# One fixed TensorE order for the RWKV stage of a hybrid recurrent layer on Trainium2, and weight splits of 1024 columns

## The chip, the cores and the metric

The kernel runs on one core of a Trainium2 chip. The metric is the device time of one launch in microseconds (us): the median of 3 runs was 2476.36 us (2475.43 to 2477.71).

Engine names follow the profile: PE is TensorE (matmuls), PEld its weight loads, DVE is VectorE, ACT ScalarE, POOL GpSimd, SP the queue that issues the DMAs. Each engine takes its instructions in the order in which they were laid down when the kernel was built, and an instruction that waits holds back those behind it.

## What is computed

One step of a decoder layer for 320 token rows: 256 rows of a prompt and 8 samples of 8 rows. Cut to what matters:

```
h    = rmsnorm(x)                     # 320 x 2048
proj = h @ w_in                       # 2048 -> 4096 (HGRN) + 3328 (RWKV) + 3072 (conv) + 6144 (gates)
y_a  = hgrn2(proj[:, HGRN]) @ w_pa
y_b  = rwkv7(proj[:, RWKV]) @ w_pb    # 16 heads of 64
y_c  = (sb * conv3(sc * sh)) @ w_pc   # short gated convolution
m    = sum of sigmoid(gates) * (y_a, y_b, y_c)
x1   = x + rmsnorm(m @ w_o)
y    = x1 + rmsnorm(relu(rmsnorm(x1) @ w_ff1)^2 @ w_ff2)     # 2048 -> 8192 -> 2048
```

The RWKV-7 part is a recurrence over the tokens of each head, S_t = S_{t-1} (diag(w_t) - kk_t (a_t kk_t)^T) + v_t k_t^T with o_t = S_t r_t, followed by a group norm, a bonus term and a gate. Besides y the step returns the new states.

## The kernel before

**Dense work.** All of it is held with features on the partitions and the 320 rows on the free axis. fp32 products are made from rounded halves: `split` (L103 to L105) writes the high part of a tile on ScalarE and the remainder on VectorE. `granule` (L107) loads 512 KB of weights (128 x 1024) on the SP queue and splits them in two halves of 512 columns; raw weights, high parts and low parts have three buffers each. `dense` (L118) accumulates one tile of 128 x 320 outputs in PSUM: for each block of 128 input features three matmuls (L128 to L130: high x high, high x low, low x high). A projection, `proj`, is 16 such blocks from two granules, 48 matmuls.

**Order of the work.** A scheduler orders each engine's instructions when the kernel is built: it takes, of those that are ready by its own account of time, the one that was written first. So program order is a priority, and the order on the chip comes from the scheduler's account. In the stage described next this decides between dense blocks, which are nearly always ready, and short matmuls of dependent chains.

**The RWKV stage** (`rwkv`, L277) follows the first norm. It works on eight pairs of heads ("heads" below), j = 0 to 7, and for each there are:

- *shift_mix* (L253): three projections (k, r, v) with a mix of each row and the row before it; two more projections serve all heads.
- *front* (L333): a low-rank product for the decay and the gate a (L346), the running product of decays in each chunk of 64 rows, a sum of squares by a matmul (L368) with `rsqrt` (L161 to L166), the operands LYR and BK, then transposes of v into X (L397, L398), the bonus (L408) and the transposes BT (L417).
- *solve* (L423): the products within the chunks (L443), masked by VectorE into Nb, GB and LYR (L452 to L457); a DRAM round trip that gathers the 16 x 16 diagonal blocks on 40 partitions, 15 dependent steps of two VectorE instructions (L474, L476), the way back into Pm (L479), and two levels of transposes and products (L499, L503, L509).
- *chunks* (L513): for each of four chunks of the prompt, one after the other, Y (L543, copied by ScalarE, L546), the solved rows (L551, copied by VectorE, L553) and the next state (L555, scaled by VectorE, L561 and L563); then the same once for the sample rows (L576 to L596).
- *tail*: group norm, transposes of Od (L635), bonus, gate product (L640) and B (L641).

`rwkv` writes them down as front 0, solve 0, front 1, and then for each j: solve j+1, chunks j, `short_conv` tiles by the list `SC_ORDER`, front j+2. `short_conv` (L672) needs three projections per tile. The branch outputs B and Cb (128 x 8 x 320 each) stay in SBUF.

**After the stage** come the HGRN stage with the merges of Cb as filler, the merges of B and A, `out_mix` and the MLP. A merge needs its branch as halves bh and bl, made by `merge_split` (L918); its projection of the gate (16 blocks) comes first.

Of the kernel before, what the change touches and what calls it, by code (L numbers as in the profile page):

```python
# [9 lines left out]
F32 = mybir.dt.float32  # L10
# [73 lines left out]
SC_ORDER = ((), (0,), (1,), (2,), (3,), (4,), (5,), (6, 7))  # L84


class K:
# [19 lines left out]
    def granule(self, src, pool=None):  # L107
# [10 lines left out]
    def dense(self, granules, ah, al):  # L118
# [4 lines left out]
        for g in granules:  # L123
            hi, lo = self.granule(g)
            for k in range(8):
# [5 lines left out]
                i += 1  # L131
        return ps[:, :NT]

# [17 lines left out]
    def proj(self, n):  # L151
        w = self.io["w_in"]
        return self.dense([w[n, 0], w[n, 1]], self.xh, self.xl)

# [15 lines left out]
    def build(self):  # L170
# [46 lines left out]
        bp = self.pool("bo", ctx=xgs)  # L217
        self.B = bp.tile([128, 8, NT], F32, name="B")
        self.Cb = bp.tile([128, 8, NT], F32, name="Cb")
# [11 lines left out]
        self.merge_split(self.Cb)  # L231
# [5 lines left out]
        for src, i, w in ((self.B, 1, io["w_pb"]), (self.A, 0, io["w_pa"])):  # L237
            self.merge_split(src)
# [14 lines left out]
    def shift_mix(self, wp, n, name, packed):  # L253

        nc = self.nc
        ps = self.proj(n)
# [12 lines left out]
        xs = wp.tile([128, NT], F32, name="xs" + name, bufs=2 if name == "v" else 1)  # L269
# [7 lines left out]
    def rwkv(self, cx):  # L277
# [21 lines left out]
        for nm, cols in (("Nb", 640), ("GB0", 640), ("GB1", 640), ("LX", 256), ("Ms", 256), ("Od", 640)):  # L299
# [9 lines left out]
        for d in self.dP:  # L309
            nc.sync.dma_start(d[0:128 * 640].rearrange("(p x) -> p x", x=640), Z["Nb"])  # L310
        self.Z = Z
        xwa = self.shift_mix(w2, RWA, "k", True)
        self.L = kp.tile([128, NT], F32, name="L")
        nc.scalar.activation(self.L[0:64, :], xwa[0:64, :], AF.Tanh)
        nc.scalar.copy(self.L[64:128, :], xwa[64:128, :])
        xg = self.shift_mix(w2, RG, "v", True)
        self.Lg = kp.tile([128, NT], F32, name="Lg")
        nc.scalar.activation(self.Lg, xg, AF.Sigmoid)
# [12 lines left out]
        nc.sync.dma_start(io["o_shift"], self.shl)  # L331

    def rwkv_front(self, j, wp, w2):  # L333
# [5 lines left out]
        kx = self.shift_mix(w2, RK + j, "k", False)  # L339
        r = self.shift_mix(w2, RR + j, "r", False)  # L340
        vx = self.shift_mix(w2, RV + j, "v", True)
# [17 lines left out]
        W = w2.tile([128, NT], F32, name="W")  # L359
        V.tensor_mul(W, Wp, wt[:, 1:])  # L360
        Wi = wp.tile([128, NT], F32, name="Wi")
        V.reciprocal(Wi, W)


        sq = wp.tile([128, NT], F32, name="sq")
# [8 lines left out]
        LYR = w2.tile([128, 5, 4, 64], F32, name="LYR")  # L374
        BK = w2.tile([128, 5, 3, 64], F32, name="BK")
# [12 lines left out]
        S.copy(BK[:, :, 2, :], BK[:, :, 0, :])  # L388
        rk = wp.tile([128, NT], F32, name="rkk")
        V.scalar_tensor_tensor(rk, r, self.par("rk", j), t, ALU.mult, ALU.mult)  # L390


        X = w2.tile([128, 5, 2, 64], F32, name="X")
# [12 lines left out]

        bs = self.pa.tile([128, 512], F32, name="pa_t")
# [3 lines left out]


        BT = w2.tile([128, 5, 2, 64], F32, name="BT")
# [6 lines left out]

        return W, LYR, BK, X, BT, vx

    def rwkv_solve(self, j, front, wp):  # L423
        nc, io = self.nc, self.io
        V, G, S, T = nc.vector, nc.gpsimd, nc.scalar, nc.tensor
        W, LYR, BK, X, BT, vx = front
# [726 lines left out]
```

## Time and profile before

| | |
|---|---|
| median of 3 runs | 2476.36 us |
| profiled execution | 2475.11 us, its span 2473.3 us |
| instructions | 41923 |
| DMA | 354.94 MB, mean 144 GB/s; weights come in 512 KB transfers |
| groups of instructions | L104 on ScalarE 685.8 us of 1192 (mean 618 ns); L105 on VectorE 828.2 us of 1192 (mean 724 ns) |

How to read it: the page gives one profiled execution. A row of the view by lines names line, engine, operation, output and inputs, the shape and the count; then busy time and the mean of one; then the idle time of that engine just before them, and what ended it. A row of the waits says which engine waited at which line for which producer: total us, times, longest. "issue" is time for which the profile shows nothing waited for. Matmuls are pipelined, so one that is listed with 309 ns can be followed by the next after half of that, and the time of a PE row is no measure of what it costs. The page's RWKV stage reaches from about 30 us to 574 us.

### The profile page before, as it was taken

How to read it: one execution, taken by the hardware profiler on the slowest of the kernel's cores; microseconds unless marked ns; L12 is line 12 of the kernel's file. 1: busy time of each engine (PE TensorE's matmuls, PEld its weight loads, DVE VectorE, ACT ScalarE, POOL GpSimd, SP SyncE). 2: the span in 40 equal slices, each digit the busy share in tenths (PEclk: the TensorE clock that was granted, in tenths of full speed). 3: DMA queues.
4: the chain of work that ended last, by engine and by line, in shares of the span. 5: the costliest groups of instructions: out<-in, count | busy, mean ns of one | idle time of the engine just before them, and what ended most of it. 6: DMA issues, size and time to landing. Idle time of an engine off the chain costs nothing.

```text
span 2473.3 us, 41923 instructions
## 1 busy us (share of the span) xinstructions
PE 2425.8 (98%) x16244; PEld 2326.5 (94%) x16244; DVE 1513.2 (61%) x3102; ACT 989.9 (40%) x1919; POOL 384.4 (16%) x536
## 2 busy tenths in 40 slices
PE   8999999999999999999999999999999999999998
PEld 7888888889999999999999897999999999999997
DVE  6878888876565656655555536754555555555555
ACT  5444444434444434433444335344333333333333
POOL 5422332220000011011111334300000000000003
PEclk9999999999999999999999999999999999999999
DMA  6323333334433333344444654444444444444443
GB/s 216 118 89 107 110 116 113 119 120 147 135 136 131 138 131 130 123 155 152 151 148 149 237 180 164 143 152 151 148 152 147 153 148 151 151 148 154 146 153 128
DMA packets 131703, 354.94 MB, mean 144 GB/s; under 512 B 34864, under 2 KB 43440, under 8 KB 131504
## 3 DMA queue, kind: packets, MB, share of 16 engines
q1 hardware_dynamic: 131504, 352.25, 41.3%
q8 instruction: 129, 2.11, 0.3%
q14 instruction: 70, 0.57, 0.1%
HBM read 337.06 MB, written 15.14 MB: 142 GB/s over the span
## 4 chain that ended last, share of the span: by engine, by line
PE 89%; DVE 8%; POOL 1%; issue 1%; ACT 1%; DMA 0%; SPq 0%; ACTq 0%; DVEq 0%; POOLq 0%
PE mm_t L128 26%; PE mm_t L130 26%; PE mm_t L129 26%; DVE wlo_t L105 1%; PE pi L443 1%; PE pi L503 1%; PE pho_t L836 1%; PE plv_t L796 1%; DVE x L972 1%; PE plv_t L797 1%; PE pi L509 0%; DVE hl L974 0%; DVE xl L200 0%; DVE Pd L476 0%; PE py_t L551 0%
## 5 line engine op out<-in xcount | busy, mean ns | idle before, releaser
L104 ACT CAST whi_t<-raw 128x512 fp32r<-128x512 f32 x1192 | 685.8, 618 | 1167.7 <-PE mm_t L129 735.5
L105 DVE TENSOR_TENSOR wlo_t<-raw,whi_t 128x512 fp32r<-128x512 f32 x1192 | 828.2, 724 | 309.2 <-ACT whi_t L104 299.4
L128 PE MATMUL mm_t<-xh,whi_t 128*128 128x320 f32 x2080 | 653.5, 314 | 0.0
L130 PE MATMUL mm_t<-xh,wlo_t 128*128 128x320 f32 x2080 | 651.3, 313 | 0.8 <-DVE wlo_t L105 0.8
L129 PE MATMUL mm_t<-xl,whi_t 128*128 128x320 f32 x2080 | 649.8, 312 | 0.0
L128 PEld LDWEIGHTS mm_t<-xh,whi_t 128*128 128x128 f32 x2080 | 391.8, 188 | 4.9 <-issue 1.8
L130 PEld LDWEIGHTS mm_t<-xh,wlo_t 128*128 128x128 f32 x2080 | 391.7, 188 | 2.6 <-DVE wlo_t L105 1.0
L129 PEld LDWEIGHTS mm_t<-xl,whi_t 128*128 128x128 f32 x2080 | 391.9, 188 | 2.0 <-issue 0.4
L128 PE MATMUL mm_t<-hh,whi_t 128*128 128x320 f32 x1232 | 381.5, 310 | 0.0
L130 PE MATMUL mm_t<-hh,wlo_t 128*128 128x320 f32 x1232 | 380.7, 309 | 0.0
L129 PE MATMUL mm_t<-hl,whi_t 128*128 128x320 f32 x1232 | 380.7, 309 | 0.0
L130 PE MATMUL mm_t<-rh,wlo_t 128*128 128x320 f32 x1024 | 316.4, 309 | 0.0
L128 PE MATMUL mm_t<-rh,whi_t 128*128 128x320 f32 x1024 | 316.4, 309 | 0.0
L129 PE MATMUL mm_t<-rl,whi_t 128*128 128x320 f32 x1024 | 316.4, 309 | 0.0
L128 PEld LDWEIGHTS mm_t<-hh,whi_t 128*128 128x128 f32 x1232 | 231.5, 188 | 6.4 <-ACT sqt L986 4.9
L129 PEld LDWEIGHTS mm_t<-hl,whi_t 128*128 128x128 f32 x1232 | 231.6, 188 | 0.0
L130 PEld LDWEIGHTS mm_t<-hh,wlo_t 128*128 128x128 f32 x1232 | 231.4, 188 | 0.0
L129 PEld LDWEIGHTS mm_t<-rl,whi_t 128*128 128x128 f32 x1024 | 192.2, 188 | 0.0
L128 PEld LDWEIGHTS mm_t<-rh,whi_t 128*128 128x128 f32 x1024 | 192.2, 188 | 0.0
L130 PEld LDWEIGHTS mm_t<-rh,wlo_t 128*128 128x128 f32 x1024 | 192.2, 188 | 0.0
L1055 DVE TENSOR_TENSOR m<-m,mm_t 128x320 f32<-128x320 f32 x112 | 54.7, 488 | 189.3 <-PE mm_t L130 189.3
L987 POOL TENSOR_TENSOR ssf<-ssf,sqt 128x320 f32<-128x320 f32 x14 | 14.1, 1004 | 841.5 <-issue 809.3
(413 smaller groups left out, 2726.8 us busy)
## 6 DMA issues: line engine op xcount, KB each, us to landing
raw<-w_in SPq DMA_DIRECT2D x260, 512.0 KB
raw<-w_ff SPq DMA_DIRECT2D x256, 512.0 KB
raw<-w_o SPq DMA_DIRECT2D x32, 512.0 KB
hs<-s_hg SPq DMA_DIRECT2D x16, 512.0 KB
raw<-w_pc SPq DMA_DIRECT2D x16, 512.0 KB
raw<-w_pb SPq DMA_DIRECT2D x16, 512.0 KB
raw<-w_pa SPq DMA_DIRECT2D x16, 512.0 KB
o_hgs<-hsn SPq DMA_DIRECT2D x16, 256.0 KB
```

Of the source, the lines that this page charges most:

```text
L104: self.nc.scalar.copy(hi, src)
L105: self.nc.vector.tensor_sub(lo, src, hi)
L128: mmul(ps[:, :NT], hi[:, w], ah[:, i, :], start=(i == 0), stop=False)
L129: mmul(ps[:, :NT], hi[:, w], al[:, i, :], start=False, stop=False)
L130: mmul(ps[:, :NT], lo[:, w], ah[:, i, :], start=False, stop=(i == n - 1))
L443: T.matmul(pp[h][:, i, :], BK[rows, c, h:h + 2, :].rearrange("p a w -> p (a w)"), LYR[rows, c, h:4:2, :], start=True, stop=True)
L503: T.matmul(ps[:, half(i)], Nb[:, i, :], cols(Mm[:, i, :], h, 0), start=True, stop=True)
L796: T.matmul(ps[:, 0:64], KS[:, 0:128], rh[:, 0:hb], start=True, stop=True)
L797: T.matmul(ps[:, 64:128], KS[:, 128:256], rh[:, hb:2 * hb], start=True, stop=True)
L836: T.matmul(op[:, 256:320], s0[:, b, :], QX[:, 64 * b:64 * b + 64], start=(b == 0), stop=False)
L972: nc.vector.scalar_tensor_tensor(x1, t, self.par("g2", k), x1, ALU.mult, ALU.add)
L1055: nc.vector.tensor_add(d, d, ps)
```

## The change

It does three things.

1. *TensorE's order in the RWKV stage is written by hand.* The stage's parts become generators that stop (`yield`) after each step, and dense work stops after each block of three matmuls (`dense_steps`). `rwkv` runs 137 slots under `manual_schedule` for TensorE alone, which then keeps the order written there; the other engines are scheduled as before. In slot t the head j takes its next step of a chain when t - 12 (j+1) is in that chain's list: front at -6, -4, 0, 1, 2; solve at 0, 1, 8 and 14 to 19; sample at 16 to 19; chunks at 21 to 32; tail at 33, 38, 40. Then come dense blocks: 7 per slot in the first 12 slots, after that the remaining 716 of 800 spread evenly. Steps of solve, chunks and sample are traced with a priority higher by 1000. The order of dense work itself is new too (`rwkv_dense`): k, r, v of each head, and conv tiles in thirds between them.
2. *A weight granule is split by one instruction of 1024 columns on each engine* instead of two of 512 (everywhere in the kernel).
3. *Buffers.* B and Cb go to DRAM tile by tile (dB, dC) and are loaded again in `merge_split` through two buffers; in SBUF, W, X, LYR, BT, the mixed v, GB and Nb get more buffers, BK fewer. The sample rows become a chain of their own with PSUM tiles from the pool `pa`.

```diff
+NSLOT = 12
+URGENT = 1000
+FRONT = (-6, -4, 0, 1, 2)
+SOLVE = (0, 1, 8, 14, 15, 16, 17, 18, 19)
+SAMPLE = (16, 17, 18, 19)
+CHUNK = tuple(range(21, 33))
+TAIL = (33, 38, 40)
...
-        for q in range(2):
-            c = slice(512 * q, 512 * q + 512)
-            self.split(hi[:, c], lo[:, c], raw[:, c])
+        self.split(hi, lo, raw)
...
+                i += 1
+                if i < n:
+                    yield
...
-        st = [self.rwkv_front(0, wp, w2)]
-        self.rwkv_solve(0, st[0], wp)
-        st.append(self.rwkv_front(1, wp, w2))
-        for j in range(8):
-            if j < 7:
-                self.rwkv_solve(j + 1, st[j + 1], wp)
-            self.rwkv_chunks(j, st[j], wp, w2)
-            for i in SC_ORDER[j]:
-                self.short_conv(i)
-            if j < 6:
-                st.append(self.rwkv_front(j + 2, wp, w2))
...
+        blocks = 50 * 16
+        chains = ((front, FRONT), (sample, SAMPLE), (chunk, CHUNK), (solve, SOLVE), (tail, TAIL))
+        total = 8 * NSLOT + TAIL[-1] + 1
+        with self.tc.manual_schedule(engines={mybir.EngineType.PE}):
+            done = 0
+            for t in range(total):
+                for j in range(8):
+                    for chain, slots in chains:
+                        if t - NSLOT * (j + 1) in slots:
+                            if chain in (chunk, solve, sample):
+                                with self.tc.high_priority(offset=URGENT):
+                                    next(chain[j], None)
+                            else:
+                                next(chain[j], None)
+                while done < max(7 * min(t + 1, NSLOT), blocks - (blocks - 7 * NSLOT) * (total - 1 - t) // (total - NSLOT)):
+                    next(dense, None)
+                    done += 1
+            self.run(dense)
...
+        conv = self.conv_tiles()
+        for j in range(8):
+            for n, name in ((RK, "k"), (RR, "r"), (RV, "v")):
+                yield from mixed(j, n, name)
...
+            for _ in range((1, 0, 1, 2, 1, 1, 2, 0)[j]):
+                yield from next(conv)
+        for c in conv:
+            yield from c
...
+        nc.sync.dma_start(self.dB[j], of)
...
+        nc.sync.dma_start(self.dC[j], sb)
...
+            if wp is None:
+                t = src[:, k, :]
+            else:
+                t = wp.tile([128, NT], F32, name="bsrc")
+                self.nc.sync.dma_start(t, src[k])
```

More of the change, by code (lines that the diff above doesn't have):

```diff
@@ L131, in dense, with run @@
                 i += 1
+                if i < n:
+                    yield
         return ps[:, :NT]
+    @staticmethod
+    def run(steps):
+        while True:
+            try:
+                next(steps)
+            except StopIteration as e:
+                return e.value
+    def dense(self, granules, ah, al):
+        return self.run(self.dense_steps(granules, ah, al))
     def dense_wide(self, tiles, ah, al, psp, wpool):
@@ L216, in build @@
         self.dT = [dp.tile([128, 8], F32, name="dT%d" % j) for j in range(8)]
[L217 to L219 removed]
+        self.dB = [dp.tile([128, NT], F32, name="dB%d" % j) for j in range(8)]
+        self.dC = [dp.tile([128, NT], F32, name="dC%d" % j) for j in range(8)]
         with ExitStack() as cx:
@@ new lines, in rwkv @@
+        dense = self.rwkv_dense(w2)
+        front = [self.rwkv_front(j, wp, w2) for j in range(8)]
+        solve = [self.rwkv_solve(j, wp) for j in range(8)]
+        chunk = [self.rwkv_chunks(j, wp, w2) for j in range(8)]
+        sample = [self.rwkv_sample(j, wp) for j in range(8)]
+        tail = [self.rwkv_tail(j, wp) for j in range(8)]
+        blocks = 50 * 16
+        chains = ((front, FRONT), (sample, SAMPLE), (chunk, CHUNK), (solve, SOLVE), (tail, TAIL))
+        total = 8 * NSLOT + TAIL[-1] + 1
@@ new lines, in rwkv @@
+        with self.tc.manual_schedule(engines={mybir.EngineType.PE}):
[13 more added lines that the diff above has]
+            self.run(dense)
+            for c in front + solve + chunk + sample + tail:
+                assert next(c, 0) == 0
@@ L564, in rwkv_chunks, with rwkv_sample @@
         nc.sync.dma_start(io["o_rwp"][j], sn)
+        otm = self.st[j]["otm"]
         for h, rows in heads:
             S.copy(otm[rows, 0:4, :], ot4[rows, :, hb(h)])
+    def rwkv_sample(self, j, wp):
+        nc, io = self.nc, self.io
+        V, G, S, T = nc.vector, nc.gpsimd, nc.scalar, nc.tensor
+        W, LYR, X, BT = (self.st[j][n] for n in ("W", "LYR", "X", "BT"))
+        Z = self.Z
+        lo, hi = slice(0, 64), slice(64, 128)
+        heads = ((0, lo), (1, hi))
+        hb = lambda h: slice(64 * h, 64 * h + 64)
+        GB, Pm, flat, alpha, rho = self.rwkv_views(j)
+        s0 = wp.tile([128, 8, 64], F32, name="s0")
+        nc.sync.dma_start(s0, io["s_rw"][j])
+        otm = self.st[j]["otm"] = wp.tile([128, 5, 64], F32, name="otm", bufs=2)
+        Y = wp.tile([128, 64], F32, name="Y4")
         LX = Z["LX"].rearrange("p (b a h t) -> p b a h t", a=2, h=2, t=8)
@@ L582, in rwkv_chunks @@
         both = self.cst("bi")
-        yp = self.py.tile([128, 512], F32, name="py_t")
+        yield
+        yp = self.pa.tile([128, 512], F32, name="pa_t")
         T.matmul(yp[:, 0:128], alpha(4), flat(X[:, 4]), start=True, stop=False)
@@ L587, in rwkv_chunks @@
             S.copy(Y[rows, :], yp[rows, hb(h)])
-        up = self.py.tile([128, 512], F32, name="py_t")
+        yield
+        up = self.pa.tile([128, 512], F32, name="pa_t")
         T.matmul(up[:, 0:64], Pm[:, 4, :], Y, start=True, stop=True)
@@ L591, in rwkv_chunks @@
             V.tensor_copy(X[rows, 4, h, :], up[rows, 0:64])
-        os = self.py.tile([128, 512], F32, name="py_t")
+        yield
+        os = self.pa.tile([128, 512], F32, name="pa_t")
         T.matmul(os[:, 0:128], Z["Ms"][:, 128:256], both, start=True, stop=False)
@@ L670, in conv_setup, with conv_tiles, part @@
         self.cvo = kp.tile([128, 8, 9, 2], F32, name="cst_o")
+    def conv_tiles(self):
+        for j in range(8):
+            c = self.short_conv(j)
+            for _ in range(3):
+                yield self.part(c)
+    @staticmethod
+    def part(steps):
+        for x in steps:
+            yield
+            if x:
+                return
     def short_conv(self, j):
```

144 lines of the change are left out of this document (92 added, 52 removed).

## The prediction

> **What bounds the kernel now.** I read the page first, then busy time by stage, then the queue of waits inside the one stage that the change touches.
>
> ```profile
> PE 2425.8 (98%) x16244; PEld 2326.5 (94%) x16244; DVE 1513.2 (61%) x3102; ACT 989.9 (40%) x1919; POOL 384.4 (16%) x536
> ...
> PE 89%; DVE 8%; POOL 1%; issue 1%; ACT 1%; DMA 0%; SPq 0%; ACTq 0%; DVEq 0%; POOLq 0%
> ```
>
> TensorE is the bound: 98% busy, 89% of the chain that ended last. Whatever is won must be time in which TensorE doesn't stream. Three stretches, in the view by window (columns: PE, PEld, DVE, ACT, POOL busy, granted clock, DMA share, GB/s):
>
> ```profile
> 30.00:574.00 544.00, 521.30 (x3517) 473.52 (x3516) 435.56 (x1153) 238.93 (x503) 172.41 (x335) 0.99 0.36 117
> ...
> 1700.00:2400.00 700.00, 700.00 (x4775) 700.00 (x4775) 368.31 (x640) 251.14 (x452) 0.00 (x0) 1.00 0.43 150
> ...
> 200.00:250.00 50.00, 49.18 (x330) 43.11 (x330) 43.58 (x121) 23.73 (x51) 13.20 (x28) 1.00 0.35 111
> ```
>
> The second row is dense work alone: 700 / 4775 = 0.1466 us per matmul, no idle weight load. The first is the RWKV stage, 544 us: matmuls idle for 22.7 us, weight loads for 70.5. VectorE is 80% busy over the stage and 87% in the third row, its crowded middle. The 22.7 us are too small a measure, since a busy matmul row runs on after the next one could have started.
>
> The Trainium skill ("Trainium Kernel Development and Optimization", Performance Expectations) says the same: matmul busy time misleads, weight-load busy time is to be read. By the one, at most 22.7 us could be won, by the other 70.5; that dense work alone shows PEld at 700 of 700 speaks for the second, as a ceiling.
>
> How much of the stage is streaming:
>
> ```profile
> L128 PE MATMUL mm_t<-xh,whi_t 128*128 128x320 f32 x783 | 251.0, 321 | 0.0
> ...
> 181.98 1.10 PE pi L503 x8
> ...
> 132.83 1.73 PE pi L443 x16
> ```
>
> Three such groups of 783 are the dense part (800 blocks of three, a few not recorded): 2349 x 0.1466 = 344 us. The other 3517 - 2349 = 1168 matmuls belong to the chains of the eight heads. Two pieces of the chain of waits price them at 1.10/8 = 0.138 and 1.73/16 = 0.108 us; with 0.117 (pieces carry the end of their last matmul, so the true value lies low) that is 137 us (126 to 161 by the ends). 544 - 344 - 137 = **63 us** in which TensorE waits or switches. Who it waits for, in the weight-load queue of that stretch:
>
> ```profile
> PEld pa_t L635 <- DVE Od L625: 7.9, 8, 1.8
> PEld py_t L551 <- ACT Y L546: 6.7, 21, 0.6
> PEld pi L443 <- issue: 4.9, 12, 1.6
> PEld pa_t L417 <- issue: 3.8, 2, 3.6
> PEld py_t L589 <- ACT Y L587: 3.3, 8, 0.5
> PEld pa_t L408 <- DVE rkk L390: 3.0, 5, 0.8
> ...
> PEld mm_t L128 <- ACT whi_t L104: 0.9, 2, 0.4
> ```
>
> The waits are short and many: a chain's next matmul stands ahead of ready dense blocks before VectorE or ScalarE has delivered. "issue" rows, just under a third of the time in these rows, are what a change from dense to chain work costs anyway; I put that at a third of the 63, 21 us, and the waits that a better order can take away at **42 us**.
>
> **The change part by part.**
>
> *The fixed order.* It removes and adds no matmul. Dense work is cut into 800 blocks (0.44 us each), 7 per slot in the first 12 of 137 slots, then 716/125 = 5.7. A later slot holds 2.5 us of dense work, and 137/96 = 1.4 us of chain work plus 21/137 = 0.15 of switching when all heads overlap: 4.1 us, 49.0 us per head (12 slots). A chunk chain takes one step per slot. Its steps cost
>
> ```profile
> L546 ACT COPY Y<-py_t 64x64 f32<-64x64 f32 x64 | 13.2, 206 | 29.0 <-PE py_t L543 28.0
> ...
> L553 DVE COPY X<-py_t 64x64 f32<-64x64 f32 x64 | 14.1, 220 | 8.8 <-PE py_t L551 7.4
> ```
>
> two copies of 0.21 or 0.22 us each: 0.45 us against at least 2.5 us of dense work. So the py_t waits (L551, L589) go, unless the copies queue behind something long on their engine; the priority of 1000 puts them ahead of all that is ready, but not of what runs. L635 and L408 likewise get a slot or more of room. If all of it goes, 42 us are won.
>
> *The front chain is tight.* From slot -4 (sum of squares) to slot 0 (the solve's first product, L443) there are 4 slots, 16 us. Its long members:
>
> ```profile
> L162 DVE RECIPROCAL rn_y<-rn_t 128x320 f32<-128x320 f32 x8 | 17.1, 2138 | 0.0
> ...
> L161 ACT ACT_TABLE_LOAD x8 | 10.3, 1283 | 0.1
> ...
> L164 POOL TENSOR_TENSOR rn_t<-rn_t,sq 128x320 f32<-128x320 f32 x8 | 7.5, 934 | 0.6
> ...
> L369 DVE TENSOR_SCALAR sq<-pa_t 128x320 f32<-128x320 f32 x8 | 3.9, 490 | 4.1 <-PE pa_t L368 4.0
> ```
>
> 2.14 + 1.28 + 0.93, and about fifteen further steps over 320 columns, which I take at L369's 0.49 us: 4.35 + 7.35, about 12 us unqueued. This chain isn't urgent; chunk copies, and a weight split already running at each of its pauses, come before it: 2 to 6 us. I charge 0.75 us per head: **6 us** (bounds 0 and 8 x 2).
>
> *VectorE in the crowded middle.* Shorter slots ask the same VectorE work in less time.
>
> ```profile
> L105 DVE TENSOR_TENSOR wlo_t<-raw,whi_t 128x512 fp32r<-128x512 f32 x196 | 134.2, 702 | 15.8 <-ACT whi_t L104 13.7 <-ACT Y L546 1.1
> ...
> L693 DVE SCALAR_TENSOR_TENSOR cv<-u,p,cv 128x336 f32<-128x336 f32 x8 | 4.5, 568 | 3.5 <-ACT cv L692 3.5
> ...
> L682 DVE TENSOR_TENSOR sh<-mm_t,rs 128x320 f32<-128x320 f32 x8 | 3.9, 492 | 1.9 <-PE mm_t L130 1.7
> ```
>
> Without splits (134.2) and the conv's two steps and three evictions (2 x 4.5 + 3 x 3.9 = 20.7), 435.6 leaves 280.7 us, 35.1 per head. A split pair now takes 134.2/98 = 1.37 us; 12 slots need 68.5/8 = 8.6 of them. With 1.30 us after the change (next part) and 0.9 for conv: 35.1 + 11.1 + 0.9 = **47.1 us per 12 slots, against 49.0 of TensorE**. At TensorE's own pace VectorE would be 96% busy; the crowded row above reaches 43.58/50 = 87%. This lasts from slot 33 (first chunks) to slot 98 (last front): 65 slots, 5.4 heads. At 92%, half way between 87 and 96, a head takes 51.2 us, 2.2 more: **12 us** (0 at 96%, 5.1 x 5.4 = 28 at 87%). This is the term I am least sure of.
>
> *Splits of 1024 columns.* One instruction for two on ScalarE and VectorE:
>
> ```profile
> 30.52 1.29 DVE L105 TENSOR_TENSOR wlo_t<-raw,whi_t 128x512 fp32r<-128x512 f32 x2
> ...
> 577.96 0.69 DVE L105 TENSOR_TENSOR wlo_t<-raw,whi_t 128x512 fp32r<-128x512 f32 x1
> ...
> L105 DVE TENSOR_TENSOR bl<-Cb,bh x8: 484/485/493, 574.7 to 577.5; 128x320 fp32r<-128x320 f32 x8
> ```
>
> A pair takes 1.29 us, one alone 0.69: the second starts under the end of the first. From 320 columns (0.485) to 512 (0.69) is 1.07 ns per column; 1024 columns then take 0.69 + 512 x 1.07 = 1.24 us. An estimate from two sizes, so 0.05 to 0.07 us is saved per granule, 98 x 0.07 = 7 us of VectorE in this stage; I took 0.07 above.
>
> The Trainium skill ("VectorE: DVE Perf Modes", the section on the errata) gives an fp32 tensor_tensor (N + 151)/0.96 ns: an estimate by it is 1.224 us for 1024 columns and 2 x 0.691 for a pair, 0.158 saved, 15 us over the stage. The single 0.69 agrees, the pair's 1.29 doesn't; by the page's figure the 12 us above would be about 8.
>
> The other side: 1024 columns stand in front of an urgent copy for 1.24 us where 512 stood for 0.69, and the first block of a granule waits for the whole split. Three buffers hide the latter: L128 waited for whi_t 0.9 us in the stage. Elsewhere TensorE streams without a gap (the row 1700:2400), and faster splits bring nothing there: 0.
>
> *B and Cb through DRAM.* 16 stores of 160 KB and 16 loads, on the same SP queue as the weights. A store that waits for its product holds the weight loads behind it, as stores do now:
>
> ```profile
> SPq L599 <- ACT BT L419: 58.3, 7, 12.8
> ...
> 1392.68 5.33 DMA ht<-dT
> ...
> L105 DVE TENSOR_TENSOR bl<-B,bh x8: 477/480/483, 1049.9 to 1053.1; 128x320 fp32r<-128x320 f32 x8
> ```
>
> SP stood up to 12.8 us behind one, yet the dense blocks lost 0.9 us; I take 0. The reload of B after the HGRN stage goes through two buffers: eight loads, the splits of today (1049.9 to 1053.1 and 0.5) between them, under a gate projection of 48 x 0.1466 = 7.0 us. At 2 us per load the last block is in time; at 5.33, the slowest landing the chain shows, four rounds of 5.33 + 1 make 25 us against 7.0 + 3.5: 15 lost. Those 5.33 came in a burst of loads, so I take 0 and keep 15 for the range. More changes of ScalarE's function table at 1.28 us each would hide in its 305 idle us unless they fall into the front chain: 0.
>
> *Sum.* -42 + 6 + 12 = -24 us. The profiled execution took 2475.11 us (span 2473.3), the median is 2476.36, 1.25 above it: 2451 by the profile, **2453** for the median, the last microsecond rounded to the cautious side.
>
> **The rivals.**
>
> *All waits go.* VectorE keeps up at 96%, the front has room enough. For it: the 29 waits of L551 and L589 are at most 0.6 us each, far less than the room that a slot gives. Against: the crowded row, the fullest 50 us of the stage, has VectorE at 87%. 2476 - 42 = 2434, with cheaper switching (one group of chain work per slot) some 7 less.
>
> *The stalls only move.* Before, an early wait went with a slower clock:
>
> ```profile
> 70.00:75.00 5.00, 3.23 (x27) 2.97 (x26) 4.94 (x11) 2.29 (x6) 0.83 (x1) 1.00 0.32 105
> 75.00:80.00 5.00, 5.00 (x34) 4.46 (x32) 4.71 (x10) 1.67 (x5) 1.13 (x2) 0.66 0.63 210
> ```
>
> After 1.8 us without a matmul the clock was 0.66 over the next 5 us: (1 - 0.66) x 5 = 1.7 us more. In a fixed order a late front holds everything behind it; eight heads with a wait of 3.5 us and 1.7 us of clock give 8 x 5.2 = 42 us back: 2476, no difference. For it: the front is the chain with least room. Against: the crowded row has the clock at 1.00, so waits of that size would be new there. The Trainium skill ("TensorE: Matmul & The Clock Gate", HAM oscillation) lets the clock halve after an idle gap above some 3.4 us; here 1.8 us sufficed, so the measurement decides, on the side against the change.
>
> *VectorE becomes the bound (slower).* Two chains, chunk and front, wait for each other through one in-order VectorE queue, and a 1.24 us split or a 2.14 us reciprocal stands before the urgent copy. At 82% a head takes 57.4 us, 8.4 above TensorE's 49.0: 5.4 x 8.4 = 45, with the front's 6 it is 51 against 42: 9 slower, 2485. It breaks even at 84.5% and costs over 5 us from 83% down. For it: the stage's mean is 80%. Against: that mean contains the thin start and end.
>
> **How the numbers follow.** The forecast (5 to 38 us faster) 0.58; all waits go 0.10; stalls only move 0.15; VectorE bound 0.17. Differences under 0.2% (5 us) can't be told from none: faster 0.58 + 0.10 = 0.68, same 0.15, slower 0.17. The range for 8 in 10: 2430 leaves out the cheaper-switching end of the first rival, 2486 most of what lies past 82% and the 15 us of slow reloads. The forecast alone has 2438 to 2471.
>
> **What would show it.** The stretch to the last gate product (L640's line) near 520 us instead of 544, PEld idle in it down from 70.5 to under 50; waits of py_t gone; VectorE above 90% in slices between 150 and 400 us; the 1024-column split at 1.2 to 1.3 us; no change in dense stretches. Wrong if VectorE's slices stay at 87% while TensorE's waits are still some 60 us, if the clock dips appear once per head, or if time is lost after the HGRN stage.

## The result, and the profile after

The changed kernel takes **2492.49 us** (median of 4 runs, 2491.54 to 2493.36) against 2476.77 for the kernel before on the same chip: ratio 1.0065, 95% interval 1.005 to 1.008. It is 16 us slower, where 23 us faster was forecast and 2486 was the end of the range.

The page of the kernel after, busy time and the chain that ended last:

```profile
PE 2417.9 (97%) x16244; PEld 2340.7 (94%) x16244; DVE 1464.6 (59%) x2506; ACT 935.9 (38%) x1325; POOL 388.1 (16%) x538
...
PE 88%; DVE 8%; issue 1%; POOL 1%; DMA 1%; ACT 0%; SPq 0%; DVEq 0%; POOLq 0%; ACTq 0%
```

TensorE does the same 16244 matmuls. That PE busy fell and PEld busy rose while the time grew tells little; where the time went shows by stage. The HGRN stage begins with its first transposes; in the trace before and in the trace after:

```profile
600.51 0.27 PE L767 MATMUL ptr_t<-c,hv 128*128 128x128 f32 x1
```

```profile
612.56 0.27 PE L891 MATMUL ptr_t<-c,hv 128*128 128x128 f32 x1
```

So 12.1 of the 16.5 us by which the span grew (2473.3 to 2489.8) are lost in the RWKV stage. From there to the end of the merges' products (those with bh and bl, the branch A's last) it is 789.7 against 786.8, in the rest 1087.5 against 1086.0. The dense stretches are as they were. The stage as a whole before (from 30 us to those transposes), then after with two more stretches (columns: PE, PEld, DVE, ACT, POOL busy, granted clock, DMA share, GB/s):

```profile
30.00:600.50 570.50, 547.80 (x3697) 500.02 (x3696) 453.24 (x1194) 252.98 (x530) 174.52 (x337) 0.99 0.37 120
```

```profile
30.00:612.60 582.60, 537.81 (x3699) 514.93 (x3698) 453.54 (x1085) 246.13 (x428) 171.48 (x339) 0.96 0.40 124
...
200.00:250.00 50.00, 45.30 (x316) 42.19 (x316) 39.99 (x113) 19.65 (x38) 10.01 (x22) 0.97 0.38 121
1700.00:2400.00 700.00, 700.00 (x4775) 700.00 (x4774) 353.64 (x436) 234.45 (x257) 0.00 (x0) 1.00 0.43 150
```

Four things are to be seen. Weight loads idle as long as before (70.5 us, now 67.7). Matmuls idle twice as long (22.7, now 44.8). The granted clock fell from 0.99 to 0.96. VectorE's busy time in the stage didn't change (453.24, now 453.54), and in the crowded stretch it is busy for 39.99 of 50 us, less than the 43.58 before.

The starts of the matmuls in the trace split this up. Of the stage's length, 507 us are streaming in both (dense x 0.1466, chains x 0.117). The 63 us left before (the prediction's 63; behind 574 us there is hardly any) are now 75. A pause is counted from one start to the next:

| us in the stage | before | after |
|---|---|---|
| pauses of TensorE above 0.5 us, less 0.3 each | 19.5 | 43.6 |
| half of the time at half clock | 3.4 | 23.9 |
| the rest: short waits and switching | 40.5 | 7.8 |

The change did what it was made for: short waits and switching fell by 33 us. It gave 24 back in long pauses and 20.5 in the clock. (The half-clock stretches after hold 4.6 us of the pauses, so 2.3 of the 23.9 are counted twice, and the last row is that much too low.) The view of waits shows the exchange, TensorE in the stage before and then after (total, times, longest):

```profile
PE pa_t L635 <- DVE Od L625: 5.8, 7, 1.5
PE pa_t L417 <- DVE t L474: 3.3, 1, 3.3
PE pi L443 <- DVE GB L455: 2.5, 2, 1.4
```

```profile
PE pi L507 <- DVE BK L446: 10.3, 4, 5.9
PE pa_t L737 <- DVE Od L726: 7.6, 4, 2.9
PE pa_t L481 <- DVE o L739: 6.0, 4, 2.4
PE mm_t L138 <- DVE wlo_t L114: 5.2, 1, 5.2
PE pi L507 <- DVE gv L715: 4.3, 2, 2.9
```

The waits on Y are gone. In their place are few and long ones, above all before L507, the solve's first product (L443 before). Two further rows name gt (3.5) and gr (2.3) at L507; these and gv are small instructions of the tail's group norm. L507 doesn't need them; they only stand next behind BK on VectorE, as at head 3:

```profile
209.74 0.49 DVE L446 SCALAR_TENSOR_TENSOR BK<-rn_y,a 128x320 f32<-128x320 f32 x1
210.15 0.17 DVE L715 TENSOR_SCALAR gv<-gv 128x5 f32<-128x5 f32 x1
...
210.38 2.32 PE L507 MATMUL pi<-LYR,BK 64*128 64x128 f32 x16 [1.37 <-DVE gv L715]
```

L507 starts 0.15 us after the end of BK. All these rows are one wait, that for the front's BK: 10.3 + 4.3 + 3.5 + 2.3 = 20.4 us.

### The profile page after: what moved, and what is told of

It reads as the page before. It is cut to its first block, busy times and chain, and to the rows that moved or that the text cites. A ratio compares the mean times of both kernels' runs of the same rounds, so it can differ in the third digit from the quotient of the medians.

```text
span 2489.8 us, 40824 instructions
## 1 busy us (share of the span) xinstructions
PE 2417.9 (97%) x16244; PEld 2340.7 (94%) x16244; DVE 1464.6 (59%) x2506; ACT 935.9 (38%) x1325; POOL 388.1 (16%) x538
## 4 chain that ended last, share of the span: by engine, by line
PE 88%; DVE 8%; issue 1%; POOL 1%; DMA 1%; ACT 0%; SPq 0%; DVEq 0%; POOLq 0%; ACTq 0%
PE mm_t L136 27%; PE mm_t L138 26%; PE mm_t L137 26%; DVE wlo_t L114 1%; PE pi L507 1%; PE pho_t L960 1%; PE pi L572 1%; PE plv_t L920 1%; DVE x L1101 1%; DVE rn_y L188 1%; PE pi L579 0%; PE plv_t L921 0%; DVE hl L1103 0%; DVE xl L226 0%; PE wide_t L761 0%
## 5 line engine op out<-in xcount | busy, mean ns | idle before, releaser
L113 ACT CAST whi_t<-raw 128x1024 fp32r<-128x1024 f32 x596 | 625.3, 1050 | 1223.0 <-PE mm_t L137 1037.6
L114 DVE TENSOR_TENSOR wlo_t<-raw,whi_t 128x1024 fp32r<-128x1024 f32 x596 | 754.4, 1267 | 431.9 <-ACT whi_t L113 430.3
L136 PE MATMUL mm_t<-xh,whi_t 128*128 128x320 f32 x2080 | 663.2, 319 | 0.0
L137 PEld LDWEIGHTS mm_t<-xl,whi_t 128*128 128x128 f32 x2080 | 397.0, 191 | 0.8
L1116 POOL TENSOR_TENSOR ssf<-ssf,sqt 128x320 f32<-128x320 f32 x14 | 19.2, 1372 | 835.8 <-ACT sqt L1115 835.8
```

Source lines behind the costliest of these rows:

```text
L113: self.nc.scalar.copy(hi, src)
L114: self.nc.vector.tensor_sub(lo, src, hi)
L136: mmul(ps[:, :NT], hi[:, w], ah[:, i, :], start=(i == 0), stop=False)
L137: mmul(ps[:, :NT], hi[:, w], al[:, i, :], start=False, stop=False)
```

## Experiments

Three causes were set against each other: **room** (the fixed order leaves too few slots between the front's sum of squares and L507), **VectorE's load** (VectorE is nearly as loaded as TensorE, and a fixed order turns each of its delays into a pause), and **long splits** (1024 columns stand in front of urgent copies). The clock is a price on top of any of them.

### More room for the front

Experiment 1 starts the front's first two steps one slot earlier:

```diff
-FRONT = (-6, -4, 0, 1, 2)
+FRONT = (-7, -5, 0, 1, 2)
```

> The changed kernel with the first two front steps one slot earlier (FRONT = -7, -5, 0, 1, 2), nothing else. Theory 1, too little room: between the sum of squares and the solve's first product TensorE has 69 dense matmuls (10.1 us) and at most 17 chain matmuls (2.0 us), 12 us and not the 16 of the prediction, and the chain needs 15 to 18; one slot more gives about 3.2 us, so the waits of L507 (2 to 4 us in six heads, 5 to 6 in the first two) shrink to under 1 us in those six and about 2 in the first two, and the half-clock spells that follow them go: 25 us of waits and some 14 of clock, 2492 - 35 = 2457 (2450 to 2470). Theory 2, VectorE is full: its slices between 100 and 450 us stay at 80 to 87%, other waits take the place, 2485 to 2492. Theory 3, the long splits hold up the copies: the wait goes but in part, about 2480.

Measured: 2479.37 us, ratio 1.0013 (1.0003 to 1.0022). That is short of the 2450 to 2470 of the room theory, yet the stage ends at 600.5, just where it ended before the change. So 13 of the 16 us hung on one slot of room, and the pauses right before L507 fell from 20.2 to 0.6 us. But pauses came up elsewhere; TensorE's waits in the stage:

```profile
PE mm_t L138 <- DVE wlo_t L114: 15.0, 8, 5.3
PE pa_t L481 <- DVE o L739: 7.8, 5, 2.3
PE pi L507 <- DVE GB L519: 7.2, 8, 1.1
PE pi L507 <- DVE BK L446: 1.1, 2, 0.5
```

The wait for BK fell from 20.4 to 1.1, and the dense blocks now wait for their low halves (15.0; 5.2 in the kernel after, 0.8 in the kernel before). Long pauses are 35.1 us still and the clock 18.8.

Experiment 6 moves the first step further ahead (to -9, the second at -5).

> FRONT = -9, -5, 0, 1, 2: the sum of squares one slot earlier as in the run with -7 and -5 (2479.4), and the decay step, whose 2.1 us reciprocal stood in VectorE's queue ahead of the front chain, two slots earlier still. Theory 1 (room and queue of this one chain): the rest of L507's waits (14 us there) halves, clock spells drop from 11 windows to some 7, 2465 to 2473. Theory 2 (VectorE full): nothing gained, the waits of dense blocks for wlo_t (17 us there) grow instead, 2477 to 2484.

Measured: 2479.19 us, ratio 1.0017 (1.0008 to 1.0026), as experiment 1; the stage ends at 600.2. More room at the front bought nothing further: long pauses are 41.3 us, 6 more than in experiment 1, and the clock 11.9, 7 less.

Experiment 4 keeps the slots after the change, and gives the front's steps the priority that chunks, solve and sample have:

```diff
-                            if chain in (chunk, solve, sample):
+                            if chain in (front, chunk, solve, sample):
```

> The changed kernel with the front's steps traced at the same raised priority as solve, chunks and sample. Theory 1: the chain is as long as before but queues less behind the group norm of the tail and behind splits (in one head 2.4 us of splits and 2.2 us of tail work ran inside it); L507's waits fall by 2 to 3 us per head, and most clock spells with them: 2465 to 2475. Theory 2: the tail and the conv wait instead, 2485 to 2492. Theory 3: 2485.

Measured: 2494.05 us, ratio 1.0072 (1.0055 to 1.0089). No help in the time, but not for want of effect: the wait for BK fell from 20.4 to 12.3 us (10.9, and 1.4 under gv's name), and that for Od grew from 7.6 to 14.3, that for low halves from 5.2 to 7.2 and that for X (L614, L628) from 4.2 to 7.1.

### The long splits

Experiment 2 is the kernel after with pairs of 512 columns, experiment 3 the kernel before with 1024; these lines change sides:

```diff
-        self.split(hi, lo, raw)
+        for q in range(2):
+            c = slice(512 * q, 512 * q + 512)
+            self.split(hi[:, c], lo[:, c], raw[:, c])
```

> The changed kernel with the old splits of 512 columns in pairs. Theory 3 (a split of 1024 columns in front of each urgent or front instruction is what made it slower): 2475 to 2480, L507's waits halved. Theory 1 (room): each of the front chain's pauses is filled by half as long a split, 1 to 2 us less wait per head, but VectorE and ScalarE work more: 2483 to 2493. Theory 2 (VectorE full): 7 us more VectorE work in the stage, 2493 to 2499.

> The kernel before with splits of 1024 columns, its order as the scheduler gives it. Theories 1 and 2: the splits matter little, within 5 us of 2476.8, a little faster in the stage by theory 2 (7 us less VectorE work: 2470 to 2477). Theory 3: 5 to 15 us slower, 2482 to 2492, with longer waits of the py_t products.

Measured: experiment 2 2494.43 us (ratio 1.0067, 1.005 to 1.0084), experiment 3 2486.48 (1.0041, 1.0026 to 1.0056). In the new order the long splits aren't the cause of the lost time: without them the wait before L507 is 13.9 us instead of 20.4, but that for low halves 12.5 instead of 5.2, and the stage is 2.9 us longer. In the old order they cost 10 us, 7.7 in the stage, as much as the third theory gave, though the waits on Y that it named are no longer (6.5 us in the weight-load queue, before 6.7). So a split's length matters by what TensorE's order puts behind it, and the two parts of the change can't be priced apart and added.

### The clock

Experiment 5 puts 20 matmuls that nothing reads ahead of each head's first product, 160 in all, in the kernel after:

```diff
+                if n > 1 and h == 0:
+                    for _ in range(20):
+                        T.matmul(ps[:, :NT], self.xh[:, 0, 0:128], self.xh[:, 0, :], start=True, stop=True)
```

> The changed kernel with 20 matmuls more per head (128x320, rounded halves, 2.9 us), written into the PSUM tile of the solve's first product just before that product, which overwrites it: useless work in the place of the wait of L507; no result changes. It adds 8 x 2.9 = 23 us of TensorE work, of which some 21 lie in waits of 2.1 to 5.8 us. If the half-clock spells behind these waits (10 windows of 3.4 us, 17 us lost) are caused by the idle time and cost what they seem to, they go, and the kernel with more work is faster: 2476 to 2486. If the spells cost nothing of their own, 2492 to 2497. If the wait of L507 sets nothing because VectorE is full, the added work shows in full: 2505 to 2516.

Measured: 2490.62 us, ratio 1.0058 (1.0043 to 1.0073). With 23.5 us more to do (160 x 0.147, the median from one start to the next in the trace) the kernel takes 2 us less. The stage by the same count: work +23.5, long pauses 43.6 to 27.4, half clock 23.9 to 11.9, the rest as before; sum -4.7, and the stage is 4.2 shorter (608.4). Without the clock's 12 us it would have come out some 8 longer. It did less than was expected of a full repair (2476 to 2486): five half-clock stretches stayed.

How a pause becomes a half-clock window shows in the kernel after in steps of 3.413 us, the length in which its clock records come. First two steps at head 3, then four at head 7:

```profile
217.94:221.35 3.41, 2.03 (x14) 1.76 (x13) 3.34 (x11) 0.56 (x1) 0.00 (x0) 1.00 0.24 96
221.35:224.77 3.42, 2.25 (x20) 1.97 (x21) 2.24 (x7) 0.81 (x2) 0.88 (x2) 1.00 0.60 165
```

```profile
432.96:436.38 3.42, 3.42 (x26) 3.36 (x25) 3.37 (x8) 1.05 (x1) 1.66 (x2) 1.00 0.44 140
436.38:439.79 3.41, 2.12 (x15) 1.62 (x13) 3.28 (x8) 0.97 (x4) 1.30 (x3) 1.00 0.41 153
439.79:443.20 3.41, 1.54 (x17) 1.29 (x17) 3.27 (x6) 1.49 (x6) 1.34 (x2) 1.00 0.14 49
443.20:446.62 3.42, 3.42 (x14) 3.42 (x14) 3.13 (x8) 1.18 (x2) 0.00 (x0) 0.50 0.42 153
```

A pause of 2.0 us that fell across two steps (with one of 0.7 behind it) left TensorE 59% and 66% busy, and the clock stayed. One of 2.9 us, with a short one ahead of it, left 62% and 45%, and the step after the 45% ran at half clock: 14 matmuls where 26 fit.

### VectorE's load

Experiment 7 is experiment 1 with every third low half of the stage's weights made by GpSimd:

```diff
+        if self.n_gran < 100 and self.n_gran % 3 == 2:
+            self.nc.scalar.copy(hi, raw)
+            self.nc.gpsimd.tensor_sub(lo, raw, hi)
```

> FRONT = -7, -5, 0, 1, 2 and every third of the stage's 100 weight splits has its low half subtracted by GpSimd instead of VectorE: 33 x 1.24 = 41 us less VectorE work in the stage, some 33 x 3 = 100 us more for GpSimd (171 of 544 now). Theory 2 (VectorE full): the waits for wlo_t and L481 shrink to a few us and clock spells with them, 2477 - 20 = 2455 to 2468. Theory 1 alone: VectorE had room, 2475 to 2482. If GpSimd's slow subtracts come too late or slow VectorE down, dense blocks wait for them, 2485 and more.

Measured: 2494.47 us, ratio 1.0074 (1.0059 to 1.0089), 15 us slower than experiment 1. It didn't test what it should, as the groups of instructions show; experiment 1 first, then experiment 7:

```profile
L726 DVE TENSOR_TENSOR Od<-otm,gr 64x320 f32<-64x320 f32 x16 | 7.8, 487 | 0.3
...
L415 DVE TENSOR_TENSOR_SCAN Wp<-sg,c 128x320 f32<-128x320 f32 x8 | 6.5, 817 | 2.3 <-POOL sg L413 2.2
```

```profile
L125 POOL TENSOR_TENSOR wlo_t<-raw,whi_t 128x1024 fp32r<-128x1024 f32 x32 | 77.4, 2418 | 60.0 <-ACT whi_t L124 36.2 <-PE py_t L628 11.9 <-PE pa_t L742 9.9
```

```profile
L731 DVE TENSOR_TENSOR Od<-otm,gr 64x320 f32<-64x320 f32 x16 | 10.4, 648 | 0.3
...
L420 DVE TENSOR_TENSOR_SCAN Wp<-sg,c 128x320 f32<-128x320 f32 x8 | 8.7, 1090 | 2.7 <-POOL sg L418 2.7
```

GpSimd takes 2.42 us for what VectorE did in 1.22. The means of VectorE's own instructions are up by a third (487 to 648 ns, 817 to 1090), but not because each took longer. The view by tile has smallest, middle and largest time:

```profile
L420 DVE TENSOR_TENSOR_SCAN Wp<-sg,c x8: 806/815/3008, 49.9 to 422.5; 128x320 f32<-128x320 f32 x8
```

Seven of the eight scans took as long as ever; one began during a subtraction on GpSimd and ended after it. There are 18 such VectorE instructions in the trace, each 1.4 to 2.2 us over the median of its kind, 35 us in all. So the load was not taken off: with some 40 us of splits gone, VectorE was still busy for 454.5 us in the stage (to 615.9), against 454.2 in experiment 1 (to 600.5).

Experiment 9 leaves the load and changes only its order: experiment 1, with the stage's splits ahead of all chain work.

```diff
+        if self.n_gran < 100:
+            with self.tc.high_priority(offset=2 * URGENT):
+                self.split(hi, lo, raw)
```

> The kernel with the front started one slot earlier (2479.4 us), with one thing more: the splits of the stage's first 100 weight blocks stand ahead of all chain work on ScalarE and VectorE. In the kernel it builds on, TensorE waits 15.0 us in 8 places for a block's low half. Order theory (VectorE has the room, the splits only stand behind chain work that could wait): these waits go, and with them three or four of the nine half-clock windows, 1.7 us each; 2460 to 2470. Theory 2 (VectorE is full, 82 to 89% in the stage): the waits move to the chains' copies (the products' masks L519, the chunk products L625 and L634, the output L739); 2476 to 2486. The number that decides is the sum of TensorE's waits in the stage, now 34 us by the view of waits, beside the time.

Measured: 2509.13 us, ratio 1.0128 (1.0113 to 1.0143), 30 us slower than experiment 1 and 23 beyond what either theory gave. TensorE's waits:

```profile
PE mm_t L141 <- DVE Rv L293: 9.7, 2, 5.0
PE pa_t L742 <- DVE Od L731: 7.8, 3, 3.0
PE pi L512 <- DVE GB L524: 7.0, 6, 1.8
PE pi L512 <- DVE BK L451: 6.4, 3, 3.0
```

Of the 15 us of waits for a low half 0.6 are left, and everything else waits; long pauses come to 51.8 us and the clock to 39.3. The theory that the splits merely stood in the wrong order has fallen.

Experiments 8 and 10 belong to what follows the stage. Experiment 8 is experiment 1 with 512-column pairs after the first 100 blocks of weights; experiment 10 adds this to experiment 8:

```diff
-                t = wp.tile([128, NT], F32, name="bsrc")
+                t = wp.tile([128, NT], F32, name="bsrc", bufs=6)
```

> FRONT = -7, -5, 0, 1, 2, with 1024-column splits for the stage's first 100 granules and pairs of 512 after it. The HGRN stage (first to last transposes and norm products) took 436.0 us in both kernels with 512 columns and 439.1 to 439.3 in all three with 1024: it should be 436 again, and the whole 3 us less than with -7 and -5 alone: 2476. If those 3 us came from the new order's end or the reload of B, no change, 2479.

> The kernel with the early front and 512-column splits after the stage (2481.4 us), whose reload of the second branch's rows gets 6 buffers in place of 2. There, the stretch from the end of the HGRN stage to the end of the third branch's products took 355.8 us against 350.5 in the kernel it builds on, with a wait of 2.6 us for a reloaded row's high half and a half-clock window of 3.4 us at 1064. If the reload is late because each row waits for one of two buffers, both go: 2475 to 2478, and that stretch takes 350 to 351. Rival: the rows come late because the high halves can be overwritten only after the last product that reads the first branch's; then the wait stays and the time too, 2479 to 2483.

Measured: 2481.4 us, ratio 1.002 (1.0011 to 1.003), and 2476.89 us, ratio 1.0001 (0.9991 to 1.001). In experiment 8 the reload of B through two buffers came late, after the HGRN stage:

```profile
PE mm_t L139 <- ACT bh L113: 2.6, 1, 2.6
```

With six buffers this wait is gone, and 4.5 us with it. The runs of experiment 8 scatter (2473.6 to 2485.3), but the two traces, with the same end of the stage, differ by 4.9 us too. From the stage's end to the end of the merges' products experiment 10 takes 786.9 us, the kernel before 786.8, experiment 1 789.4: 512 columns and six buffers together are worth 2.5 us there. Experiment 10 is the kernel before in time, with the same end of the stage, and a good base for the rest.

Experiment 11 gives room at its two next places; experiment 12 moves the front's first step to -9 as well:

```diff
-FRONT = (-7, -5, 0, 1, 2)
-SOLVE = (0, 1, 8, 14, 15, 16, 17, 18, 19)
+FRONT = (-7, -5, 0, 1, 3)
+SOLVE = (0, 2, 8, 14, 15, 16, 17, 18, 19)
```

> The kernel with the early front, the 512-column splits after the stage and the 6 reload buffers (2476.9 us), with room at two more places of the slot table: the solve's second group of products goes from slot 1 to slot 2, since it waits for the masks of the first group to empty the same two buffers (7.2 us in 8 places), and the front's last transposes go from slot 2 to slot 3, since they wait for the tail's output to empty theirs (7.7 us in 5 places). Room theory (the fixed order lacks room at single places, and a wait of over 1 us there also brings a half-clock window): those 15 us of waits go and four of the nine half-clock windows in which one of them has a part, 1.7 us each; 2453 to 2462. Theory 2 (VectorE is the bound, and what is taken away at one place turns up at another): the sum of long waits stays about 35 us; 2472 to 2480.

> The same, with the front's first step at slot -9 in place of -7. With the step there (in the kernel of 2479.2 us) the wait of 5.3 us for a block's low half at the second head was gone, and half-clock windows in the stage came to 23.9 us against 37.5. Room theory: a further 5 to 8 us less than the kernel beside it; 2447 to 2457. Theory 2: the same as the kernel beside it within 3 us.

Measured: 2481.51 us (ratio 1.0022, 1.0013 to 1.0032) and 2484.88 (1.0032, 1.0019 to 1.0045). In experiment 11 the waits for GB and for o, 15 us, are gone. The wait for low halves has taken them over, from 14.7 us in 7 places in experiment 10:

```profile
PE mm_t L141 <- DVE wlo_t L114: 29.4, 14, 5.6
```

Experiment 12 has fewer of those (14.1), and in their place one of 7.1 us for Pm's way back from DRAM. Room moves a pause; by then it no longer removes one. Leaving out some of the weight splits does. Experiment 14 is experiment 10, experiment 15 the kernel after, each with every third low half of the stage's first 100 blocks left out: the products read the low half of the block before.

```diff
+        if self.n_gran < 100 and self.n_gran % 3 == 2:
+            self.nc.scalar.copy(hi, raw)
+            return hi, self.last_lo
```

> The same kernel with every third low half of the stage's first 100 weight blocks left out: its products read the low half of the block before, so 33 subtractions, about 42 us of VectorE work by 1.28 us each, are gone and TensorE's order stays. Not the reference's numbers. Theory 2: the time falls by most of that, as far as waits and half-clock windows reach (54 us in the stage); 2435 to 2455. Room theory: 2470 to 2478.

> The kernel after, with the same third of the low halves left out. Theory 1 (too little room between the sum of squares and the first product): the front's chain still has 12 us of TensorE's work for a chain of some 12 us, so 3 us of wait a head and its window stay; 2480 to 2490. Theory 2: with a tenth less to do VectorE gets through the chain sooner; 2450 to 2470.

Measured: 2458.26 us (ratio 0.9923, 0.9908 to 0.9939) and 2476.78 (1.0002, 0.9993 to 1.0011): 18.6 less than experiment 10, 15.7 less than the kernel after. TensorE's order and its matmuls are the same as without the omission. The stage in experiment 10, then 14, then 15:

```profile
30.00:600.50 570.50, 535.33 (x3700) 511.03 (x3699) 456.05 (x1096) 247.45 (x439) 174.28 (x339) 0.97 0.42 128
```

```profile
30.00:584.00 554.00, 528.28 (x3700) 505.84 (x3699) 419.13 (x1062) 246.62 (x438) 163.40 (x338) 0.98 0.43 133
```

```profile
30.00:596.40 566.40, 532.91 (x3700) 510.44 (x3699) 418.23 (x1052) 246.09 (x428) 164.02 (x338) 0.97 0.42 128
```

37 us less of VectorE's time (456.05 to 419.13) shorten the stage by 16.5. Experiment 14 came out 3 us above what the load theory gave (2435 to 2455) and far from the room theory's 2470 to 2478, experiment 15 between the two (2450 to 2470, and 2480 to 2490). In experiment 15 the pauses right before L507 still add up to 19.5 us of the 20.2 in the kernel after (both from the starts of the matmuls): that place lacks room with the smaller load too. The other long pauses fell from 23.4 to 12.4 us, and the clock from 23.9 to 17.1.

These two runs change two things at once, for a block whose low half is left out doesn't wait for one either. In experiment 14 that matters: of the 9.9 us by which its long pauses are shorter than in experiment 10, waits for low halves make 7.9. In experiment 15 they make only 3.3 (5.2 to 1.9) of 11.7, and the wait for Od alone fell by 6.7 (7.6 to 0.9), so there the load counts by itself.

Experiment 13 is a kernel that computes everything: experiment 10 with plain copies and scalings on ScalarE instead of VectorE (the sample's too).

```diff
-                V.tensor_copy(X[rows, c, h, :], up[rows, 0:64])
+                S.copy(X[rows, c, h, :], up[rows, 0:64])
...
-                    V.tensor_scalar_mul(dst, sp[rows, hb(h)], wc[rows])
+                    S.activation(dst, sp[rows, hb(h)], AF.Copy, scale=wc[rows])
...
-        V.tensor_scalar(t, a, self.par("ka", j), self.omka[:, j:j + 1], ALU.mult, ALU.add)
+        S.activation(t, a, AF.Identity, scale=self.par("ka", j), bias=self.omka[:, j:j + 1])
```

> The kernel of 2476.9 us (early front, 512-column splits after the stage, 6 reload buffers), with plain copies and scalings taken from VectorE to ScalarE: the chunks' and the sample's copies X (64 and 16), the first chunk's scaled copies (16), the sample's Ms (16) and the front's tk (8), by its own rows some 30 us of VectorE in the stage, 4 us a head of 48. ScalarE has the room (246 us busy of 570). Theory 2 (VectorE's load holds TensorE): a head's 57 us falls by up to the 4 us, and half-clock windows with it; 2445 to 2465. Room theory: no change, 2472 to 2480; slower if the copies queue behind ScalarE's weight halves.

Measured: **2473.46 us**, ratio 0.9984 (0.9976 to 0.9993): 3 us under the kernel before and 19 under the kernel after, though under the 0.2% that the prediction took for measurable. The stage:

```profile
30.00:596.80 566.80, 529.78 (x3701) 507.35 (x3700) 426.84 (x976) 276.07 (x559) 172.85 (x339) 0.97 0.43 129
```

VectorE has 29 us less to do and ScalarE 29 more; the stage is 3.7 us shorter, an eighth of it, where leaving splits out gave nearly half. It fell short of the 2445 to 2465 expected: waits for low halves even grew from 14.7 to 17.7 us. So it isn't VectorE's busy time as such that TensorE pays for: the copies taken away here weren't what stood in front of the splits. That is inferred from the waits; no run tests it alone.

## Why the prediction was wrong, step by step

**What bounds the kernel: right.** TensorE with 63 us of waits and switching in the stage; the long stretches of dense work stayed as they were.

**The fixed order, -42: right in kind, near in size.** Short waits and switching gave 33 us. Y's waits are gone, as forecast; those for X (L614, L628) are not quite, at 4.2 us. The 21 us that were kept as the price of switching, from the "issue" rows, were too many: after the change 7.8 us are left of short waits and switching together. Such rows can be waits: the largest of the weight-load queue after the change is L507's, 24.2 us, the place of the wait for BK.

**"The front chain is tight", 6 us: this is the step that failed.** It took "4 slots, 16 us" from the mean slot of 4.1 us. The slots from -4 to 0 aren't mean ones. In the trace after TensorE has 66 to 69 dense matmuls there (10.1 us) and 3 to 17 of the chains (2.0 us at most): 12 us, just the unqueued length of the chain by the prediction's own sum. From the sum of squares to L507 it took 14.8 to 18.3 us, so the "2 to 6 us" of queueing were about right. But nothing was left to cover them, and the charge should have been the whole of it and not 0.75. The pauses right before L507 in the eight heads are 5.8, 0.1, 1.5, 1.3, 2.3, 3.5, 2.9 and 2.7 us, 20.2 in all where 6 were charged and 16 was the bound. With other pauses in the same slots it is 29.6 (the second head's 5.3 is a wait for a low half). Experiment 1 shows what the place was worth: one slot more, and 13 us come back, 12 of them in the stage. The stage was forecast 24 us shorter and came out 12 longer; the other 24 of these 36 us belong, as far as the runs tell, to the next two terms.

**The clock: left out of the sum, and under-sized in the rival.** "The stalls only move" had the mechanism and its place. It priced the clock at 8 x 1.7; the trace has 12 half-clock stretches in the stage, 47.8 us long, half of which is 23.9 against 3.4 before. "If the clock dips appear once per head" was named as what would prove the forecast wrong, and they did, at every head from the third on. Its 42 us are near the 24.1 + 20.5 = 44.6 that were lost so; it gave no difference because it set them against the whole 42, and the gain was 33. The argument against this rival, a clock of 1.00 in the crowded row, was about a kernel whose pauses were still spread out. The loss by the count is more than the whole slowdown of the stage. It is worked out, not isolated: experiment 5 took half of it away, and no run keeps the pauses and loses the clock.

**VectorE in the crowded middle, 12 us: the direction right, the reading too mild.** The balance of 47.1 us against 49.0 per head holds in the counts; the period of a head came out at 58 us in the last four, not 51.2. VectorE never reached the 92% (39.99 to 43.72 us in each 50 between 150 and 400): pauses of TensorE hold VectorE up too, since its work comes from TensorE. Two engines with nearly equal work that wait for each other many times per head didn't run at the pace of the busier one here. Experiments 11 and 9 show pauses moving between VectorE's customers; in experiment 14, 37 us less of its work gave 18.6, in experiment 13 another 29 us gave only 3.4. The rival "VectorE becomes the bound" comes nearest, with 2485: it had two chains that wait for each other through VectorE's queue, and at 82% a head of 57.4 us, where VectorE was 83.5% busy from 150 to 400 us and a head took 58. It still fell 7.5 us short. It put the whole of a longer head down to VectorE, while part of it is the clock; and its other 6 us were for a front that cost 20.

**Splits of 1024 columns: their size right, their effect not.** The page has them at

```profile
L114 DVE TENSOR_TENSOR wlo_t<-raw,whi_t 128x1024 fp32r<-128x1024 f32 x596 | 754.4, 1267 | 431.9 <-ACT whi_t L113 430.3
```

against 1.24 estimated and 1.2 to 1.3 asked for; the middle one took 1.225, and the 14 in the stage above 1.4 us all ran beside GpSimd's work. The 7 us were VectorE's time; in the stage's length the long splits are worth 2.9 us in one trace (experiment 2), and the whole kernel's times don't tell them apart. "Three buffers hide the latter" held for high halves; for low halves TensorE waited 5.2 us, and 15.0 in experiment 1. "Elsewhere 0" holds for the dense stretches. The HGRN stage, from its first transposes to its last product, took 441.5 to 442.0 us in the nine traces with 1024 columns there and 438.4 to 438.6 in the eight with 512: 3 us that the prediction had at nothing. Why is open.

**B and Cb through DRAM, 0 with 15 kept for the range:** 0.7 us of waits for bh and bl in the kernel after; at another phase of the loads 2.6 (experiment 8).

**The sum** was -42 + 6 + 12 = -24. Measured: -33 for short waits and switching, +24 for long pauses and +20.5 for the clock make +12 in the stage, with 2.9 up to the end of the merges and 1.5 behind: 16.5. Three of the tests asked for failed: the last gate product came at 582 us, not 550; PEld idled 67.7 us, not under 50; VectorE stayed under 90%.

**What stays open:** how an early front would do with splits of 512 columns in the stage, which no run has; why the stage's VectorE order, with the same load, puts the pauses where it does (no run fixed it by hand as the change fixed TensorE's), and how far the clock's share would go if the same idle time lay in short pieces.

## What to carry to other kernels

Before an order is fixed by hand, count the work that really lies between two steps of each dependent chain, slot by slot, and compare it with the chain's length including its queueing; a mean slot hides the thin ones. A scheduler's many short waits can be cheaper than a fixed order's few long ones, because a pause that empties a clock window is paid once as a wait and again as half speed. When waits move from place to place as each is given room, stop moving them and look at the engine that they all name: what helped here was less of the work that stood in front of the awaited results, not less work of any kind.

## What the runs showed of the hardware

**The clock goes by fixed windows.** Over all 17 traces of this case the stretches between the clock records were cut into steps of 3.413 us. For each step at full clock, TensorE's busy share in it (the profile's own, with modelled ends) was set beside the clock of the step behind it. Under 40% busy, all 109 were followed by half clock; from 40 to 50% 45 of 60; from 50 to 60% 33 of 77; from 60 to 70% 11 of 82; above 70% none of 11693. (Where exactly the cuts lie moves a count by one or two.) So 1 us of pause alone in a step, which leaves 71%, never cost speed; two of 1.2 and 1.3 us in one step did (experiment 6, at 270 us), and 2 us did or didn't by where they fell. The Trainium skill ("TensorE: Matmul & The Clock Gate", What's actually happening) has a free-running activity window of 4096 cycles, about 3.4 us; the records agree with 3.413 us. Its rule of no idle gap above some 3.4 us (HAM oscillation) is too lenient here: a third of a window without work could do it.

**GpSimd beside VectorE.** In experiment 7 the subtractions on GpSimd took 2.42 us each by the profile's spans. The 18 VectorE instructions named there all began during one of them and ended 0.02 to 0.7 us after its end, so a scan of 0.82 us became one of 3.01. Those beside a subtraction that read a tile in PSUM kept their time, and so did the reciprocals (2.15 us). The Trainium skill ("Perfetto Trace Analysis", Optimizing Scalar/DVE Operations) says that these two share a read port of SBUF, so that moving work between them might not help; experiment 7 agrees, with 15 us lost.
